# RWKV layer: the keys' input kept in SBUF as two parts, 1024-wide weight splits, no mask on the key products, factors padded to 112 rows, and weight loads issued by ScalarE

## The chip, the cores and the metric

The kernel runs on one core of one Trainium2 chip. The metric is the device time of one execution in microseconds (us): the median of three runs, and beside it one execution that was profiled. TensorE multiplies matrices, VectorE and GpSimd do elementwise work, ScalarE does activations, casts and copies, and SyncE (SP) issues most DMAs. Each engine takes its instructions in an order that is fixed when the program is built; DMAs of one issuing engine are issued in that engine's order too.

## The reference

Two layers over 256 positions of 2048 channels, in float32. Layer 0 mixes positions with Hyena and gated linear attention, layer 1 with RWKV-7; each is followed by a squared-ReLU feed-forward layer, and everything is modulated by a condition vector. The change lies in the RWKV block:

```python
xr, xw, xk, xv, xa, xg = [h + xx * mu[j] for j in range(6)]
r, k, v = heads(xr @ w_r), heads(xk @ w_k), heads(xv @ w_v)
kk = normalised(k * k_k)                            # per head of 64
for d in range(2):                                  # forward, backward
    logw = -0.606531 * sigmoid(w0[d] + tanh(xw @ w1[d]) @ w2[d])
    a = sigmoid(a0[d] + (xa @ a1[d]) @ a2[d])
    k_d = k * (1 + (a - 1) * k_a)
    state_out += rwkv7_scan(r, logw, k_d, v, kk, a)  # a state of 64x64 per head
    bonus += sum(r * k_d * r_k) * v
o = (groupnorm(state_out) + bonus) * g
return o @ w_o
```

## The kernel before

**Products in float32.** A factor `a` of a large product is split into `hi` (a cast to a TensorE format, by ScalarE, L466) and `lo = a - hi` (by VectorE, or GpSimd for inputs, L467). `prod` (L502) issues three matmuls, hi x hi, hi x lo and lo x hi (L505 to L507). A weight tile is 128 x 2 x 512 (512 KB); `load` (L488) takes it from DRAM with a DMA of SyncE into the pool `wp` of six buffers, which the background loads of the modulation weights (`ada`, L314 to L363) share.

**The order of the work.** The stages are generators; `weave` (L945) interleaves their steps by given counts, and a scheduler then fixes each engine's order from a simulated timeline. `issue_after(ins)` puts what is traced within it behind `ins` in its engine's order.

**The RWKV layer**, L1100 to L1271, in stages:

- *Norm and mixes.* `norm_steps` writes h; `xx` is the difference of the neighbours' mean and h. `spill_mixes` (L1275) makes the inputs of k, r and v, mixes 2, 0 and 3, two channel tiles (128 x 512 values) at a time with VectorE, and stores each to DRAM (`mix0`, `mix2`, `mix3`) with a DMA of SyncE. Beside it run the small projections (`lora`, L1284) and the first 35 steps of the projections.
- *Projections.* `rwkv_linear` (L1021) makes 512 output channels of k, r or v. It takes its tiles from `stream` (L994): for each of eight steps it loads an input tile `xu` (256 KB) back from DRAM, casts it (ScalarE) and subtracts (GpSimd), loads the next weight tile, and splits the present one in two halves of 512 columns (`split_weights`, `W1 = W2 = 2`). One input tile serves 24 matmuls. The same input is loaded and split again for each of the four blocks of output channels.
- *Keys.* In four rounds (L1171) the projections k and r of the next block run beside `rwkv_keys` (L1326) for the 16 pairs of heads, two lanes at a time, and `invert` (L1405) for the block before. Each two pairs load one tile of factors `up`, [97, 4, 256] (388 KB, L1180): 96 rows of w2 and a2 and a row of biases. For each direction `rwkv_keys` makes the decay (L1342 to L1344), `a` (L1347 to L1350), two tiles u0, u1 (VectorE and GpSimd), the cumulated decays (L1363 to L1365), the scaled factors `ab` (VectorE, L1374 to L1377, two products of 256 columns for the two tiles u), the products of 64 positions with each other (L1387), masked to the part below the diagonal by VectorE (L1393, `nm`), and stores them in `nd` and `ab` (L1394, L1395). `invert` reads `nd` in blocks of 32 rows (L1413) and uses the entries below the diagonal alone; `pair_load` reads back the blocks beside the diagonal.
- *Chain of states.* For pair after pair: `pair_load`, `pair_prep`, `pair_chain`, `pair_tail`, beside the other three blocks of v, then the output projection (`rwkv_out`, L1048). At the end (L1261) the last tile of each of the four output blocks is loaded, split, multiplied, and added to the residual.

The names in the profile: `tm_w`, `tm_wh`, `tm_wl` are a weight tile and its parts, `tm_xu`, `tm_xh`, `tm_xl` an input tile and its parts, `tm_up` the factors, `f_` the feed-forward layers, `tm_mm` and `tm_ps` PSUM tiles.

Of the kernel before, what the change touches and what calls it, by code (L numbers as in the profile page):

```python
# [16 lines left out]
P = 128  # L17
# [13 lines left out]
LG, MK, XS, TB, DU, RP, IB, L1, MP, AP = 2, 7, 4, 0, -8.0, 1, 3, 0, 3, 5  # L31
W1, W2, X1, X2 = 2, 2, 1, 1
BG, IV, CH, MT, B0, B1, M0, M1, LD = (10, 10, 10, 10, 10, 10, 10, 10, 10, 5, 5, 5, 5, 5, 5, 5, 5, 5), 12, 7, (5, 5, 5, 5, 5, 5, 5, 5, 5, 5, 5, 2, 3, 2, 3, 2, 3, 2), 3, 14, 6, 6, 6
PK = 8
RH, ZZ = (0, 2.4, 2, 2), 0
# [73 lines left out]
def _rwkv_constants():  # L109
    o = {}  # L110
    for d in range(2):
        st = _block_tri(64, True, d == 1)
        inc = _block_tri(64, False, d == 1)
        o[f"cum{d}"] = np.concatenate([st, inc], axis=1) * np.float32(-0.606531)
        st64, inc64 = st[:64, :64], inc[:64, :64]
        z = np.zeros((64, 64), np.float32)
        top = np.concatenate([z, inc64], axis=1)
        bot = np.concatenate([st64, inc64], axis=1)
        o[f"mm{d}"] = np.concatenate([bot, top] if d else [top, bot], axis=0)
    lower = np.tril(np.ones((64, 64), np.float32), -1)  # L120
    o["nm"] = np.concatenate([lower, lower], axis=0)
    h = np.arange(P) // 64
    o["bo"] = (h[:, None] == h[None, :]).astype(np.float32)
    return o


def layout(i):
# [56 lines left out]
    for n, v in _rwkv_constants().items():  # L184
        (rk1 if n[:3] in ("cum", "nm") else rk).add(n, v)
    a["rc"], a["rc1"] = rk.array(), rk1.array()
# [7 lines left out]
    for w, b in (("rw_w2", "rw_w0"), ("rw_a2", "rw_a0")):  # L194
        w, b = np.asarray(i[w])[0], np.asarray(i[b])[0]
        for d in range(2):
            up.append(np.concatenate([w[d], b[d][None]], axis=0))
    a["rw_up"] = np.stack(up, axis=1).reshape(97, 4, 8, T).transpose(2, 0, 1, 3)
    a["rw_g2"] = np.asarray(i["rw_g2"])[0].reshape(2, P, 4, NB).transpose(2, 1, 0, 3)
# [15 lines left out]
class Build:  # L215
# [21 lines left out]
    def run(self):  # L237
        nc, ctx, A = self.nc, self.ctx, self.A
        self.const = self.pool(ctx, "const")
        self.wp = self.pool(ctx, "wp", bufs=6)  # L240
        self.due, self.rate, self.turn, self.hold, self.starting = 0.0, 0.0, 0, None, False
        self.cut = None
# [12 lines left out]
        self.ada_next, self.ada_sum, self.ada_out, self.ada_done = [], {}, {}, {}  # L255
        self.label = self.stages[0]
        if self.stages[0] != "mix":
            self.start()
            self.load_x()
        for s in SUBS:  # L260
            if s in self.stages:
                self.label = s
                self.rate = RF0 if s == "f0" else RF1
                if s[0] == "f":
                    self.ffn(s)
                elif s == "mix":
                    self.mix()
                else:
                    self.rwkv()
        self.final()  # L270
# [194 lines left out]
    def split(self, a, hi, lo, eng=None):  # L465
        self.nc.scalar.copy(hi, a)  # L466
        d = (eng or self.nc.vector).tensor_tensor(lo, a, hi, ALU.subtract)  # L467
        if eng is None:
            self.cut = d.ins

    def behind(self):
# [16 lines left out]
    def load(self, name, n, i, pools):  # L488

        self.turn += 1  # L490
        w = self.t(pools[self.turn % len(pools)], [P, 2, NB], "w")
        self.dma = self.nc.sync.dma_start(w, self.A[name][n, i // 2][:, i % 2 * 2 : i % 2 * 2 + 2]).ins
        self.tick(self.rate / 2)
        return w
# [487 lines left out]

    def open_linear(self, st, bufs, fine, finex):
        self.fine, self.finex = fine, finex
        self.ws = self.pool(st, self.name("ws"), bufs=bufs, reuse_waits="tile")
        self.xt = self.pool(st, self.name("xt"), bufs=bufs, reuse_waits="tile")
# [7 lines left out]
    def stream(self, name, n, src, tiles):  # L994

        nc = self.nc
        w = [self.load(name, n, 0, [self.wp])]

        def ahead(i):
            u = self.t(self.xt, [P, 2, T], "xu", bufs=2)  # L1000
            nc.sync.dma_start(u, src[:, 2 * i : 2 * i + 2, :])
            x = [self.t(self.xt, [P, 2, T], t, dt=F32R) for t in ("xh", "xl")]
            for j in range(self.finex):
                c = slice(j * T // self.finex, (j + 1) * T // self.finex)
                self.split(u[:, :, c], *(a[:, :, c] for a in x), nc.gpsimd)
            if 2 * i + 2 < tiles:
                w.append(self.load(name, n, i + 1, [self.wp]))
            v = [self.t(self.ws, [P, 2, NB], t, dt=F32R) for t in ("wh", "wl")]
            self.split_weights(w[i], v)
            return x, v  # L1010
# [3 lines left out]
        for i in range(tiles // 2):  # L1014
            x, v = nxt
            if 2 * i + 2 < tiles:
                nxt = ahead(i + 1)
            for k in range(2):
                yield 2 * i + k, [a[:, k, :] for a in x], [a[:, k, :] for a in v]

# [79 lines left out]
    def rwkv(self):  # L1100
# [3 lines left out]
        xs = tc.dram_tile([P, 2, D], F32, name="x_spill")  # L1104
        self.xd = {j: tc.dram_tile([P, KT, T], F32, name=f"mix{j}") for j in (0, 2, 3)}
        yd = tc.dram_tile([P, KT, T], F32, name="y_spill")
# [6 lines left out]
        with ExitStack() as st:  # L1113
# [15 lines left out]
            st1 = st.enter_context(ExitStack())  # L1129
            self.open_linear(st1, 3, W1, X1)  # L1130
            rk = self.pool(st1, "rk", reuse_waits="tile")
# [17 lines left out]
            with ExitStack() as st2:  # L1149
# [11 lines left out]
                self.xstack.close()  # L1161
                self.rate = 0.0
                mixes = self.spill_mixes(h, xx)
# [5 lines left out]
            with st1:  # L1169
                p1 = self.pool(st1, "p1", reuse_waits="tile")  # L1170
                for n in range(4):  # L1171
# [3 lines left out]
                    def lane(o):  # L1175
                        for i in range(2):
                            p = 4 * n + 2 * i + o
                            if o == 0:
                                up[i] = self.t(p1, [97, 4, T], "up", bufs=2)
                                nc.sync.dma_start(up[i], A["rw_up"][p // 2])  # L1180
                            c = p % 4
                            yield from self.rwkv_keys(p1, p, r[:, c, :], k[:, c, :], kk[:, c, :], kh[:, c, :], up[i][:, :, o * P : (o + 1) * P])

# [6 lines left out]
            with ExitStack() as st1:  # L1190
                self.open_linear(st1, 2, W2, X2)
                p2 = self.pool(st1, "p2", reuse_waits="tile")
# [68 lines left out]
                for n in range(4):  # L1261
# [9 lines left out]
                    self.residual("tm", n, pts[n])  # L1271
        self.open_gate()
        self.open_work()

    def spill_mixes(self, h, xx):  # L1275
        for j in (2, 0, 3):
            for k in range(0, KT, 2):
                u = self.t(self.tmp, [P, 2, T], "u")
                for q in range(2):
                    self.mixed(h, xx, j, k + q, u[:, q, :])  # L1280
                self.nc.sync.dma_start(self.xd[j][:, k : k + 2, :], u)
                yield 1
# [43 lines left out]
    def rwkv_keys(self, rp, p, r, k, kk, kh, up):  # L1326
# [11 lines left out]
        for d in range(2):  # L1338
# [5 lines left out]
            Gp.tensor_scalar(sig, sig, 0.5, 0.5, ALU.mult, ALU.add)  # L1344
            th = self.t(rp, [P, T], "th", bufs=3)
            pt = self.pt([P, T])
# [5 lines left out]
            yield 1  # L1352
            u = [self.t(rp, [P, T], f"u{n}", bufs=3) for n in range(2)]
            V.scalar_tensor_tensor(u[d], th, 1.0, kh, ALU.add, ALU.mult)
            Gp.tensor_tensor(u[1 - d], sc, k, ALU.mult)
# [4 lines left out]
            en = self.t(rp, [P, T], "en", bufs=3)  # L1360
            pt = self.pt([P, 2, 2, P])
# [12 lines left out]
            V.tensor_tensor(ar[:, 0, :], ar[:, 0, :], kk, ALU.mult)  # L1374
            for n in range(2):
                V.tensor_tensor(bk[:, :, n, :], c4(u[n]), c4(en), ALU.mult)
            V.tensor_tensor(ar[:, 1, :], ar[:, 1, :], r, ALU.mult)  # L1377
# [14 lines left out]
            for hd in range(2):  # L1392
                V.tensor_tensor(nt[:, hd], pts[hd], self.rc("nm").unsqueeze(1).to_broadcast([P, 2, 64]), ALU.mult)  # L1393
            nc.sync.dma_start(self.nd[b][:, d, 256 * pb : 256 * pb + 256], nt.rearrange("p h t j -> p (h t j)"))  # L1394
# [319 lines left out]
```

## Time and profile before

| | us |
|---|---|
| median of three runs (3163.99 to 3170.43) | 3164.84 |
| the profiled execution | 3173.39 |
| its span, first to last instruction | 3171.6 |
| TensorE busy (matmuls) | 2904.6 |
| VectorE busy | 2195.9 |
| ScalarE busy | 1340.4 |
| GpSimd busy | 620.7 |

A profile row names the line, the engine (PE is TensorE, PEld its weight loads, DVE VectorE, ACT ScalarE, POOL GpSimd, SP SyncE; a q behind it is its sequencer, which waits and issues DMAs), the operation, what it writes and reads, its shape and count; then its busy time, the mean of one in ns, the engine's idle time just before it and what ended that. The granted clock is the share of TensorE's full clock that it was given. Busy time of overlapping instructions counts once in the views by stretches; in the groups each instruction counts with its full length, so matmuls that overlap add up to more.

### The profile page before, as it was taken

The page shows a single profiled execution, that of the slowest core. Times are in us where ns is not written, and L with a number is a line of the kernel's source. Part 1 is how long each engine was busy: PE and PEld are TensorE (multiplying, and loading weights), DVE is VectorE, ACT ScalarE, POOL GpSimd, SP SyncE. Part 2 cuts the span into 40 slices and gives each one's busy share as a digit, 9 for nine tenths or more (in the row PEclk, how much of TensorE's full clock was granted, in tenths as well). Part 3 has the DMA queues.
Part 4 walks back from the last instruction along what each step waited for, and adds up shares of the span by engine and source line. Part 5 has one row for each costly group of instructions (what it writes and reads, how often), then busy time and mean ns, then how long its engine had stood idle before and what let it go on. Part 6 is the DMA issues. An engine that isn't in the chain of part 4 may idle for free. (4 is left out here: it accounts for less than half of the span.)

```text
span 3171.6 us, 52610 instructions
## 1 busy us (share of the span) xinstructions
PE 2904.6 (92%) x20308; PEld 2513.1 (79%) x20308; DVE 2195.9 (69%) x3350; ACT 1340.4 (42%) x2083; POOL 620.7 (20%) x646
## 2 busy tenths in 40 slices
PE   5999899999999999979577777999998999999998
PEld 2677776799988998868476676787777998899986
DVE  7899776657777787787368685975556677555554
ACT  3233444444433444433354553444445444344443
POOL 1211100021100110023355464442323110001100
PEclk9999999999999999999788897998999999999999
DMA  9978777648889888966455567896635678555552
GB/s 320 326 257 290 245 269 265 230 150 285 291 305 314 291 295 301 311 214 226 152 185 175 178 208 192 270 292 208 192 108 192 224 250 284 196 188 180 199 193 99
DMA packets 285494, 741.39 MB, mean 234 GB/s; under 512 B 73601, under 2 KB 100097, under 8 KB 284092
## 3 DMA queue, kind: packets, MB, share of 16 engines
q1 hardware_dynamic: 284668, 734.40, 69.0%
q8 instruction: 159, 2.61, 0.3%
q10 hardware_dynamic: 576, 3.64, 0.3%
q14 instruction: 91, 0.75, 0.1%
HBM read 697.23 MB, written 40.70 MB: 233 GB/s over the span
## 5 line engine op out<-in xcount | busy, mean ns | idle before, releaser
L467 DVE TENSOR_TENSOR f_wl<-f_w,f_wh 128x1024 fp32r<-128x1024 f32 x512 | 631.0, 1233 | 444.5 <-ACT f_wh L466 440.4
L466 ACT CAST f_wh<-f_w 128x1024 fp32r<-128x1024 f32 x512 | 538.4, 1052 | 748.3 <-PE f_mm L507 319.3
L506 PE MATMUL f_mm<-f_h,f_wh 128*128 128x256 f32 x2048 | 579.6, 283 | 0.0
L505 PE MATMUL f_mm<-f_h,f_wh 128*128 128x256 f32 x2048 | 579.4, 283 | 0.0
L507 PE MATMUL f_mm<-f_h,f_wl 128*128 128x256 f32 x2048 | 579.0, 283 | 0.0
L506 PE MATMUL f_mm<-f_wl,f_hid 128*128 128x512 f32 x1024 | 398.6, 389 | 0.6 <-DVE f_wl L467 0.6
L507 PE MATMUL f_mm<-f_wh,f_hid 128*128 128x512 f32 x1024 | 398.5, 389 | 0.0
L506 PEld LDWEIGHTS f_mm<-f_h,f_wh 128*128 128x128 f32 x2048 | 393.2, 192 | 0.2
L505 PEld LDWEIGHTS f_mm<-f_h,f_wh 128*128 128x128 f32 x2048 | 393.0, 192 | 0.1
L507 PEld LDWEIGHTS f_mm<-f_h,f_wl 128*128 128x128 f32 x2048 | 392.9, 192 | 0.0
L505 PE MATMUL f_mm<-f_wh,f_hid 128*128 128x512 f32 x1024 | 357.9, 389 | 0.0
L467 POOL TENSOR_TENSOR f_hid<-f_u,f_hid 128x512 fp32r<-128x512 f32 x64 | 98.0, 1531 | 990.0 <-ACT f_hid L466 985.2
L467 DVE TENSOR_TENSOR tm_wl<-tm_w,tm_wh 128x512 fp32r<-128x512 f32 x256 | 206.0, 830 | 99.0 <-ACT tm_wh L466 98.4
L363 DVE SCALAR_TENSOR_TENSOR mix_w<-mix_w,mix_s 128x1024 f32<-128x1024 f32 x175 | 219.8, 1265 | 73.3 <-DMA mix_w<-in_ada_f 49.1
L505 PE MATMUL tm_mm<-tm_xh,tm_wh 128*128 128x256 f32 x768 | 242.9, 320 | 18.5 <-ACT tm_xh L466 11.1
L506 PE MATMUL tm_mm<-tm_xl,tm_wh 128*128 128x256 f32 x768 | 234.5, 306 | 8.8 <-POOL tm_xl L467 8.8
L363 DVE SCALAR_TENSOR_TENSOR f_w<-f_w,mix_s 128x1024 f32<-128x1024 f32 x174 | 233.4, 1344 | 2.3 <-DMA f_w<-in_ada_f 2.3
L507 PE MATMUL tm_mm<-tm_xh,tm_wl 128*128 128x256 f32 x768 | 232.6, 305 | 1.4 <-DVE tm_wl L467 1.4
L467 POOL TENSOR_TENSOR tm_xl<-tm_xu,tm_xh 128x512 fp32r<-128x512 f32 x113 | 169.4, 1500 | 310.5 <-ACT tm_xh L466 268.8
L506 PEld LDWEIGHTS f_mm<-f_wl,f_hid 128*128 128x128 f32 x1024 | 192.2, 188 | 40.9 <-DVE f_wl L467 1.2
L507 PEld LDWEIGHTS f_mm<-f_wh,f_hid 128*128 128x128 f32 x1024 | 192.2, 188 | 39.8
L505 PEld LDWEIGHTS f_mm<-f_wh,f_hid 128*128 128x128 f32 x1024 | 192.3, 188 | 39.7
(445 smaller groups left out, 5413.9 us busy)
## 6 DMA issues: line engine op xcount, KB each, us to landing
f_w<-in_w SPq DMA_DIRECT2D x512, 512.0 KB, 4.9
f_w<-in_ada_f SPq DMA_DIRECT2D x125, 512.0 KB, 5.5
mix_w<-in_ada_mix SPq DMA_DIRECT2D x96, 512.0 KB, 6.4
mix_w<-in_w_in SPq DMA_DIRECT2D x80, 512.0 KB, 5.2
mix_w<-in_ada_f SPq DMA_DIRECT2D x64, 512.0 KB, 5.0
f_w<-in_ada_tm SPq DMA_DIRECT2D x49, 512.0 KB, 5.7
tm_xu<-mix SPq DMA_DIRECT2D x96, 256.0 KB, 4.8
mix_w<-in_w_out SPq DMA_DIRECT2D x32, 512.0 KB, 4.7
```

The lines of the kernel that those rows point to most:

```text
L363: V.scalar_tensor_tensor(w, w, 1.0, self.s[:, j * (D // 2) : (j + 1) * (D // 2)], ALU.mult, ALU.mult, accum_out=a[:, j, i : i + 1])
L466: self.nc.scalar.copy(hi, a)
L467: d = (eng or self.nc.vector).tensor_tensor(lo, a, hi, ALU.subtract)
L505: mm(out, lhsT=l[0], rhs=r[0], start=start, stop=False)
L506: mm(out, lhsT=l[0], rhs=r[1], start=False, stop=False)
L507: mm(out, lhsT=l[1], rhs=r[0], start=False, stop=stop)
```

## The change

- The padded factors: `rw_up` gets 15 rows of zeros, and the tile `up` is [112, 4, 256]; the products read its first 97 rows.
- The inputs: `spill_mixes` splits each mix once. The parts of the keys' input stay in two SBUF tiles (`xk`); those of r and v are stored to DRAM together, 512 KB for two channel tiles, and `stream` loads them back as they are, without a cast or a subtract.
- Weight splits are one cast and one subtract of 1024 columns (`W1 = W2 = 1`), and `stream` loads `PF = 3` weight tiles ahead of the one that it splits, not one.
- In the RWKV layer, from the spill of x to its end, `load` issues the weight DMAs from ScalarE, behind the newest cast of a weight (`casts[-1]`), and not from SyncE. This holds for the output projection too, where a load is traced one tile ahead.
- The mask is gone: ScalarE copies the products of L1387 whole.
- In `rwkv_keys` u0 and u1 are one tile, and their product with `en` is one operation over 512 columns; `th` and `en` have two buffers, not three.

```diff
-W1, W2, X1, X2 = 2, 2, 1, 1
+W1, W2 = 1, 1
-PK = 8
+PK, PF = 8, 3
...
-    a["rw_up"] = np.stack(up, axis=1).reshape(97, 4, 8, T).transpose(2, 0, 1, 3)
+    up = np.stack(up, axis=1).reshape(97, 4, 8, T).transpose(2, 0, 1, 3)
+    a["rw_up"] = np.concatenate([up, np.zeros((8, 15, 4, T), np.float32)], axis=1)
...
     def split(self, a, hi, lo, eng=None):
-        self.nc.scalar.copy(hi, a)
+        c = self.nc.scalar.copy(hi, a)
         d = (eng or self.nc.vector).tensor_tensor(lo, a, hi, ALU.subtract)
         if eng is None:
             self.cut = d.ins
+            self.casts = [c.ins]
...
-        self.dma = self.nc.sync.dma_start(w, self.A[name][n, i // 2][:, i % 2 * 2 : i % 2 * 2 + 2]).ins
+        src = self.A[name][n, i // 2][:, i % 2 * 2 : i % 2 * 2 + 2]
+        if self.wq is None:
+            self.dma = self.nc.sync.dma_start(w, src).ins
+        else:
+            with self.tc.issue_after(self.casts[-1]):
+                self.wq.dma_start(w, src)
...
-        w = [self.load(name, n, 0, [self.wp])]
+        w = [self.load(name, n, i, [self.wp]) for i in range(PF)]
 
         def ahead(i):
-            u = self.t(self.xt, [P, 2, T], "xu", bufs=2)
-            nc.sync.dma_start(u, src[:, 2 * i : 2 * i + 2, :])
-            x = [self.t(self.xt, [P, 2, T], t, dt=F32R) for t in ("xh", "xl")]
-            for j in range(self.finex):
-                c = slice(j * T // self.finex, (j + 1) * T // self.finex)
-                self.split(u[:, :, c], *(a[:, :, c] for a in x), nc.gpsimd)
-            if 2 * i + 2 < tiles:
-                w.append(self.load(name, n, i + 1, [self.wp]))
+            if isinstance(src, list):
+                x = src[i // 4][:, 2 * i % 8 : 2 * i % 8 + 2]
+            else:
+                x = self.t(self.xt, [P, 2, 2, T], "x", bufs=self.xb, dt=F32R)
+                nc.sync.dma_start(x.bitcast(F32), src[:, 2 * i : 2 * i + 2])
+            if 2 * (i + PF) < tiles:
+                w.append(self.load(name, n, i + PF, [self.wp]))
...
-            self.open_linear(st1, 3, W1, X1)
+            self.open_linear(st1, 3, W1, 3)
+            xk = self.pool(st1, "xk", reuse_waits="tile")
+            self.xd[2] = [self.t(xk, [P, 8, 2, T], f"xk{i}", dt=F32R) for i in range(2)]
...
-                self.rate = 0.0
+                self.rate, self.wq = 0.0, nc.scalar
...
-                                up[i] = self.t(p1, [97, 4, T], "up", bufs=2)
+                                up[i] = self.t(p1, [112, 4, T], "up", bufs=2)
...
-                self.nc.sync.dma_start(self.xd[j][:, k : k + 2, :], u)
+                if j == 2:
+                    x = self.xd[2][k // 8][:, k % 8 : k % 8 + 2]
+                else:
+                    x = self.t(self.hp, [P, 2, 2, T], "xs", bufs=2, dt=F32R)
+                self.split(u, x[:, :, 0], x[:, :, 1], self.nc.gpsimd)
+                if j != 2:
+                    self.nc.sync.dma_start(self.xd[j][:, k : k + 2], x.bitcast(F32))
...
-            for n in range(2):
-                V.tensor_tensor(bk[:, :, n, :], c4(u[n]), c4(en), ALU.mult)
+            V.tensor_tensor(bk, u.rearrange("p n (c t) -> p c n t", t=64), c4(en).unsqueeze(2).to_broadcast([P, 4, 2, 64]), ALU.mult)
...
-                V.tensor_tensor(nt[:, hd], pts[hd], self.rc("nm").unsqueeze(1).to_broadcast([P, 2, 64]), ALU.mult)
+                S.copy(nt[:, hd], pts[hd])
```

More of the change, by code (lines that the diff above doesn't have):

```diff
@@ L119, in _rwkv_constants @@
         o[f"mm{d}"] = np.concatenate([bot, top] if d else [top, bot], axis=0)
-    lower = np.tril(np.ones((64, 64), np.float32), -1)
-    o["nm"] = np.concatenate([lower, lower], axis=0)
     h = np.arange(P) // 64
@@ L184, in layout @@
     for n, v in _rwkv_constants().items():
-        (rk1 if n[:3] in ("cum", "nm") else rk).add(n, v)
+        (rk1 if n[:3] == "cum" else rk).add(n, v)
     a["rc"], a["rc1"] = rk.array(), rk1.array()
@@ L241, in run @@
         self.due, self.rate, self.turn, self.hold, self.starting = 0.0, 0.0, 0, None, False
-        self.cut = None
+        self.cut, self.casts, self.wq = None, [], None
         self.small = self.pool(ctx, "small", bufs=2)
@@ L981, in mixed, with open_linear @@
         self.nc.vector.scalar_tensor_tensor(o, xx[k // 8][:, k % 8, :], self.v(f"mu{j}")[:, k : k + 1], h[k // 8][:, k % 8, :], ALU.mult, ALU.add)
-    def open_linear(self, st, bufs, fine, finex):
-        self.fine, self.finex = fine, finex
+    def open_linear(self, st, bufs, fine, xb):
+        self.fine, self.xb = fine, xb
         self.ws = self.pool(st, self.name("ws"), bufs=bufs, reuse_waits="tile")
@@ L1018, in stream @@
             for k in range(2):
-                yield 2 * i + k, [a[:, k, :] for a in x], [a[:, k, :] for a in v]
+                yield 2 * i + k, [x[:, k, a] for a in range(2)], [a[:, k, :] for a in v]
     def rwkv_linear(self, name, n, j, out):
@@ L1104, in rwkv @@
         xs = tc.dram_tile([P, 2, D], F32, name="x_spill")
-        self.xd = {j: tc.dram_tile([P, KT, T], F32, name=f"mix{j}") for j in (0, 2, 3)}
+        self.xd = {j: tc.dram_tile([P, KT, 2, T], F32, name=f"mix{j}") for j in (0, 3)}
         yd = tc.dram_tile([P, KT, T], F32, name="y_spill")
@@ L1178, in lane @@
                             if o == 0:
-                                up[i] = self.t(p1, [97, 4, T], "up", bufs=2)
+                                up[i] = self.t(p1, [112, 4, T], "up", bufs=2)
                                 nc.sync.dma_start(up[i], A["rw_up"][p // 2])
                             c = p % 4
-                            yield from self.rwkv_keys(p1, p, r[:, c, :], k[:, c, :], kk[:, c, :], kh[:, c, :], up[i][:, :, o * P : (o + 1) * P])
+                            yield from self.rwkv_keys(p1, p, r[:, c, :], k[:, c, :], kk[:, c, :], kh[:, c, :], up[i][:97, :, o * P : (o + 1) * P])
                     def late():
@@ L1190, in rwkv @@
             with ExitStack() as st1:
-                self.open_linear(st1, 2, W2, X2)
+                self.open_linear(st1, 2, W2, 3)
                 p2 = self.pool(st1, "p2", reuse_waits="tile")
@@ L1271, in rwkv @@
                     self.residual("tm", n, pts[n])
+        self.wq = None
         self.open_gate()
@@ L1344, in rwkv_keys @@
             Gp.tensor_scalar(sig, sig, 0.5, 0.5, ALU.mult, ALU.add)
-            th = self.t(rp, [P, T], "th", bufs=3)
+            th = self.t(rp, [P, T], "th", bufs=2)
             pt = self.pt([P, T])
@@ L1352, in rwkv_keys @@
             yield 1
-            u = [self.t(rp, [P, T], f"u{n}", bufs=3) for n in range(2)]
-            V.scalar_tensor_tensor(u[d], th, 1.0, kh, ALU.add, ALU.mult)
-            Gp.tensor_tensor(u[1 - d], sc, k, ALU.mult)
+            u = self.t(rp, [P, 2, T], "u2", bufs=3)
+            V.scalar_tensor_tensor(u[:, d], th, 1.0, kh, ALU.add, ALU.mult)
+            Gp.tensor_tensor(u[:, 1 - d], sc, k, ALU.mult)
             ab = self.t(rp, [P, 1024], "ab", bufs=4)
@@ L1359, in rwkv_keys @@
             bk = ab[:, 512:].rearrange("p (c n t) -> p c n t", c=4, n=2)
-            en = self.t(rp, [P, T], "en", bufs=3)
+            en = self.t(rp, [P, T], "en", bufs=2)
             pt = self.pt([P, 2, 2, P])
```

## The prediction

> **What bounds the kernel now.** I read the time and the slices first, then the busy time by stretches of the RWKV layer, then who waited for whom in the worst stretch, then the SyncE queue there. In the slices the TensorE row has one long dip, slices 20 to 25, and its granted clock drops with it:
>
> ```profile
> span 3171.6 us, 52610 instructions
> PE   5999899999999999979577777999998999999998
> PEclk9999999999999999999788897998999999999999
> ```
>
> One slice is 3171.6/40 = 79.3 us, so this is about 1507 to 1982 us: the keys stage, in which the heads' factors are made (`rwkv_keys`) beside the projections k, r and the first block of v. The busy time by stretches (us, then busy us and instruction count of each engine, granted clock, DMA share, GB/s):
>
> ```profile
> 1385.00:1505.00 120.00, 103.61 (x644) 91.24 (x645) 92.68 (x165) 41.56 (x72) 44.86 (x42) 0.95 0.64 215
> 1505.00:1562.00 57.00, 30.61 (x220) 28.95 (x219) 19.46 (x32) 18.17 (x38) 18.57 (x23) 0.73 0.43 139
> 1955.00:2160.00 205.00, 196.27 (x2271) 164.67 (x2272) 156.54 (x351) 85.34 (x216) 82.19 (x96) 0.92 0.91 270
> 2160.00:2420.00 260.00, 254.07 (x2702) 194.27 (x2702) 151.87 (x325) 120.69 (x305) 73.16 (x107) 0.99 0.53 161
> 1505.00:1955.00 450.00, 319.64 (x2442) 287.68 (x2440) 300.27 (x566) 209.57 (x420) 222.92 (x276) 0.83 0.56 181
> ```
>
> The columns are TensorE, its weight loads, VectorE, ScalarE, GpSimd. The mixes (1385 to 1505) and the chain of states (1955 to 2420) have TensorE busy for 86% and 97%. In the keys stage no engine is full: TensorE has 319.6 of 450 us, VectorE 300.3, the DMA engines 56%. 130 us of TensorE are idle there, and its clock is 0.83. So this stage is bound by waits. They are, for TensorE, ScalarE and VectorE in turn (total us, times, longest):
>
> ```profile
> PE tm_ps L1387 <- DVE tm_ab L1376: 40.2, 13, 6.6
> PE tm_ps L1317 <- ACT tm_u L1315: 23.9, 3, 10.5
> PE tm_mm L1387 <- DVE tm_ab L1376: 16.3, 3, 11.5
> PE tm_ps L1342 <- DMA tm_up<-in_rw_up: 14.9, 1, 14.9
> PE tm_mm L505 <- ACT tm_bon L1401: 7.4, 1, 7.4
> PE tm_mm L505 <- ACT tm_xh L466: 5.9, 2, 3.2
> ACT tm_xh L466 <- DMA tm_xu<-mix: 124.4, 27, 14.9
> DVE tm_wl L467 <- ACT tm_wh L466: 69.0, 12, 13.5
> ```
>
> They are one chain: TensorE waits for VectorE and ScalarE, VectorE waits for ScalarE's casts, and ScalarE, which takes its instructions in order, stands for 124 us in front of the cast of an input tile `xu` that has not landed. Why a 256 KB tile lands late is in the SyncE queue (start, us to issue):
>
> ```profile
> 1505.26 5.37 SPq L1180 DMA_DIRECT2D tm_up<-in_rw_up  x2
> 1510.73 14.68 SPq L492 DMA_DIRECT2D tm_w<-in_rw_k  x1
> ...
> 1616.35 0.31 SPq L1180 DMA_DIRECT2D tm_up<-in_rw_up  x1
> 1616.76 4.40 SPq L1001 DMA_DIRECT2D tm_xu<-mix  x1
> 1621.27 13.09 SPq L1413 DMA_DIRECT2D tm_E<-nd  x4
> ```
>
> The factors' load `up` of 1616.35 is itself issued in 0.31 us. Behind it and its fellows the next issues take 14.68, 4.40 and, for four, 13.09. The first `up`, 388 KB, goes out at 1505.26; its first reader starts at 1524.6, after the 14.9 us wait shown above: 19.3 us, where a 512 KB weight tile needs 5.7 (median to landing):
>
> ```profile
> L1342 PEld LDWEIGHTS tm_ps<-tm_up,tm_hw x104: 186/192/338, 1524.6 to 1911.3; 97*128 97x128 f32 x104
> tm_w<-in_rw_r SPq DMA_DIRECT2D x32, 512.0 KB, 5.7
> tm_w<-in_rw_o SPq DMA_DIRECT2D x32, 512.0 KB, 4.5
> tm_up<-in_rw_up SPq DMA_DIRECT2D x8, 388.0 KB
> ```
>
> So `up` moves at 20 GB/s, beside 92 for a weight tile that shares the engines with others, and a stage that moves 181. I read it as a transfer that goes through one of the 16 DMA engines, with every later transfer waiting for its share of that engine. There are eight of them, one for each 56 us of the stage. The Trainium skill, "DMA: Bandwidth & Descriptors", section on why a DMA increments its semaphore by 16, has the rule for it: a transfer uses the largest number of engines up to 16 that divides its slowest dimension, so 97 rows use one and 112 would use all 16. The trace agrees for 97; for 112 no run here shows it.
>
> **The change part by part.** The rows for the terms (busy us, mean ns; the first seven of the keys stage, then a matmul of the feed-forward layers, one ScalarE issue, a wait of the SyncE queue over the RWKV layer, and a 1024-wide subtract of the feed-forward layers):
>
> ```profile
> L467 DVE TENSOR_TENSOR tm_wl<-tm_w,tm_wh 128x512 fp32r<-128x512 f32 x120 | 101.4, 869 | 69.1 <-ACT tm_wh L466 69.0
> L1376 DVE TENSOR_TENSOR tm_ab<-tm_u,tm_en 128x256 f32<-128x256 f32 x64 | 33.2, 554 | 2.4 <-POOL tm_u L1355 2.4
> L1393 DVE TENSOR_TENSOR tm_N<-tm_ps,tm_rc 128x128 f32<-128x128 f32 x48 | 12.8, 280 | 7.4 <-PE tm_ps L1387 6.4 <-PE tm_mm L1387 1.0
> L466 ACT CAST tm_wh<-tm_w 128x512 fp32r<-128x512 f32 x118 | 67.2, 621 | 18.4 <-PE tm_mm L506 18.1
> L466 ACT CAST tm_xh<-tm_xu 128x512 fp32r<-128x512 f32 x57 | 35.3, 621 | 131.1 <-DMA tm_xu<-mix 124.4 <-PE tm_mm L507 3.7 <-POOL tm_kr L1398 3.0
> L467 POOL TENSOR_TENSOR tm_xl<-tm_xu,tm_xh 128x512 fp32r<-128x512 f32 x58 | 88.6, 1530 | 151.8 <-ACT tm_xh L466 133.9 <-issue 15.3 <-DMA ab<-tm_ab 2.5
> L505 PE MATMUL tm_mm<-tm_xh,tm_wh 128*128 128x256 f32 x479 | 152.4, 321 | 13.3 <-ACT tm_bon L1401 7.4 <-ACT tm_xh L466 5.9
> L505 PE MATMUL f_mm<-f_h,f_wh 128*128 128x256 f32 x2048 | 579.4, 283 | 0.0
> L1160 ACTq DMA_DIRECT2D x_spill<-mix_x x1: 333/333/333, 1381.2 to 1381.2; - x1
> SPq L492 <- DVE tm_wl L467: 93.6, 42, 13.6
> L467 DVE TENSOR_TENSOR f_wl<-f_w,f_wh 128x1024 fp32r<-128x1024 f32 x512 | 631.0, 1233 | 444.5 <-ACT f_wh L466 440.4
> ```
>
> *Keys stage, the waits.* The factors' load gets 112 rows. Its cost afterwards lies between today's 19.3 us and that of a weight tile; I take the weight tile, 5.7, as it is the same size and kind. The inputs also stop being cast here: keys read SBUF, r and v come as finished parts, so TensorE alone waits for them and ScalarE no longer stands in front of a DMA. Of TensorE's waits above I strike the `up` load (14.9), those on ScalarE (23.9, 7.4, 5.9 = 37.2) and half of those on VectorE at L1387 (56.5/2 = 28), which VectorE owes to late casts; the other half is the lanes' own latency and stays. That is 80 us. Late next is VectorE. Its bounds: 52 us (no VectorE wait goes) and 108 (all do).
>
> *Keys stage, the clock.* A projection's matmul takes 321 ns here and 283 where TensorE runs without gaps. With 283 for 321 throughout, 319.6 us would be 282, 38 less; the gaps do not all close, so I take 15, with 0 and 38 as ends.
>
> *Keys stage, the engines' work.* VectorE: 60 weight tiles as one subtract of 1233 instead of two of 869 save 60 x 0.505 = 30 us; 64 masks of 0.28 save 18; one product over 512 for two over 256 saves about 32 x (1.108 - 0.869) = 8. It keeps 244 us, so it does not bound a stage of 355. ScalarE: 57 input casts go (-35), 64 mask copies come (at the mask's own 0.28, +18), 60 issues of 0.333 come (+20), and wider casts are at worst equal: about 213 us, no bound. GpSimd loses 88.6. All this I count at nothing beyond the waits. Two small tiles, `th` and `en`, go from three buffers to two; each is read within a step, so I count nothing, and if a lane does wait it is for one product, 0.55 us. The inputs of r and v still go through the SyncE queue, behind stores that wait for VectorE, but three tiles ahead instead of two.
>
> *Mixes, 1385 to 1505.* 24 casts and 24 GpSimd subtracts come, 16 each of the projections' own go, so +8 x 0.62 us on ScalarE and +8 x 1.53 on GpSimd, which have 78 and 75 us free beside 104 us of TensorE; 16 wider splits save 8 us of VectorE. The stores of the mixes for r and v go out one cast and one subtract, 2.2 us, later, and nothing reads them for a whole projection. I take 0, with 8 either way.
>
> *Chain of states.* TensorE is busy 97% there and loses no matmul, so cheaper splits bring nothing. Two things cost. The inputs of the three later v blocks come as 512 KB, not 256: 24 tiles, +6.3 MB in a stretch that moves 270 GB/s at a share of 0.91, so up to 297 at full share: 21 us of DMA against 18 free. I take 5, between 0 and 21. And ScalarE now issues the weight loads behind its newest cast. In the projections that cast is three tiles back, in the output's loop two; but at the end, where four output tiles follow each other, a load stands directly behind the cast of the tile before: 0.33 to issue, 4.5 to land, two casts of 0.62 make 6.1 us for a tile. Today these loads go out well ahead, the last at 2395, and are cast from 2409 on:
>
> ```profile
> 2392.90 2.48 SPq L492 DMA_DIRECT2D tm_w<-in_rw_o  x2
> ...
> 2409.30 2.18 ACT L466 CAST tm_wh<-tm_w 128x512 fp32r<-128x512 f32 x4 [4.47 <-PE tm_ps L507]
> ...
> 2414.09 1.14 ACT L466 CAST tm_wh<-tm_w 128x512 fp32r<-128x512 f32 x2 [1.14 <-PE tm_mm L507]
> ```
>
> Three tiles cast within 5.9 us become three of 6.1 each: +12; some of it hides behind the residual, so 10, between 0 and 15. What queues behind ScalarE's waits there are the copies of the chain (L1551, L1561, L1578), for which TensorE waits next.
>
> A rule against this part stands in the same page of the Trainium skill, section "Issuing engines are not separate DMA queues": a second issuing engine saves only issue time. By it the move to ScalarE earns nothing by itself; my sum credits it nothing either, and the wait at the end remains.
>
> The sum, against the profiled execution: -80 - 15 + 0 + 5 + 10 = -80 us. The profiled execution took 3173.4 (span 3171.6), 8.6 above the median of the runs, 3164.8; the difference goes on the median: 3085.
>
> **The rivals.** *The factors' load is not the cause, or stays slow*: if ScalarE's late tiles come from the order of the SyncE queue and the lanes' own latency, TensorE only gains the first wait and some of ScalarE's, about 14.9 + 25 of the 37, and pays the 15 of the chain: 3140. For it: much of the waiting stands at L1387, a short chain through three engines. Against it: the long waits of ScalarE, up to 14.9 us, are as long as the stuck issues.
>
> *VectorE becomes the bound and all waits go*: the stage shrinks to TensorE's 282 us plus the lanes' starts, about 300: -150 + 15, 3030. For it: VectorE's 244 and TensorE's 282 both fit. Against: TensorE's order is fixed and a lane passes four engines at each step.
>
> *Slower*: ScalarE inherits the wait of the SyncE queue. The weight loads waited 93.6 us there for VectorE to release a slot of the pool of six; now ScalarE stands in front of them, and behind it the cast that VectorE needs next and the copies of the chain. With all 93.6 on the path beside -80 the change ends at +14, 3179. It decides from 80 us of such waits on. Against it: the load stands behind a cast three tiles back, so its slot has usually been free for two tiles; only in the stretch 1955 to 2160, where the gate's 35 background tiles share the pool, is it tight.
>
> **How the numbers follow.** My forecast has 0.66. Its terms' ends, 28 either way for the waits, 19 for the clock and 13 for the chain, are independent and add in squares to 36, so its own range is 3049 to 3121. The small gain has 0.15, the large one 0.11, slower 0.06, and 0.02 that gains and costs meet within 0.2% (6.3 us, about what a measurement of this kernel can tell from no change). Faster is then 0.92, the same 0.02, slower 0.06. The range over the cases, leaving out slower and the far ends of the others, is 3025 to 3145.
>
> **What would show it.** In the profile after, `up` should land within some 6 us and no issue behind it should take over 3; ScalarE's wait for `mix` tiles should be gone; slices 19 to 24 should show TensorE at 8 or 9 and a clock near 0.9; the keys stage should last about 355 us, the chain about 480, with a gap in TensorE before the last four output tiles. I am wrong if ScalarE shows long waits in front of weight loads, if TensorE's waits at L1387 stay at 56 us, or if the chain's stretch grows by more than 30 us.

## The result and the profile after

| | before | after |
|---|---|---|
| median, us, on one chip | 3166.76 | 3079.90 |
| ratio, 95% interval | | 0.972 (0.970 to 0.974) |
| the profiled execution, us | 3173.39 | 3078.22 |
| its span, us | 3171.6 | 3076.4 |

The forecast was 3085. Three disturbed executions count in the medians but not in the ratios: one of the changed kernel (3230.86 us, at a clock of 0.835), and one each of e1 and e5 below (4637.7 and 9578.1 us); without them the medians are 3079.2, 3118.1 and 3069.5.

The page of the changed kernel: the span, and the rows of TensorE and of its granted clock in 40 slices of 76.9 us.

```profile
span 3076.4 us, 51944 instructions
PE   5998989999999999998999969899998999999998
PEclk9999999999999999998999988799999999999999
```

The long dip of slices 20 to 25 is gone. A short one is left in slices 24 to 26 (TensorE 6, 9, 8, clock 8, 8, 7), 1769 to 2000 us: the end of the keys stage and the first two fifths of the chain.

To compare stages exactly I cut at TensorE's own landmarks: the first matmul of the norm, the last of `lora`, the first and the last of the line with which `pair_chain` begins (L1549 before, L1561 after), and the first of the next norm.

| stage, us | before | after | difference |
|---|---|---|---|
| mixes | 118.4 | 119.7 | +1 |
| keys | 453.0 | 324.8 | -128 |
| chain of states | 394.2 | 419.0 | +25 |
| output tail | 75.6 | 81.5 | +6 |
| feed-forward after it | 743.3 | 743.8 | 0 |

The busy time by stretches for keys, chain and tail (us; then busy us and count of TensorE, its weight loads, VectorE, ScalarE, GpSimd; granted clock, DMA share, GB/s), before:

```profile
1505.00:1958.00 453.00, 319.64 (x2442) 287.68 (x2440) 300.43 (x566) 209.57 (x420) 223.87 (x278) 0.83 0.56 181
1958.00:2353.00 395.00, 386.43 (x4645) 310.51 (x4646) 266.82 (x613) 174.03 (x458) 137.84 (x189) 0.95 0.73 217
```

and after:

```profile
1507.30:1832.10 324.80, 280.66 (x2412) 257.26 (x2410) 240.89 (x409) 184.20 (x362) 150.14 (x218) 0.95 0.81 260
1832.10:2251.20 419.10, 391.20 (x4650) 314.35 (x4651) 256.58 (x581) 160.43 (x408) 103.62 (x170) 0.91 0.70 212
2251.20:2332.60 81.40, 67.72 (x329) 50.63 (x329) 39.78 (x59) 36.73 (x60) 18.93 (x15) 0.94 0.59 193
```

Two subtractions in each row say what happened. Keys: TensorE's idle time fell from 453.0 - 319.6 = 133 us to 324.8 - 280.7 = 44, and its busy time by 39, for the same matmuls at a clock of 0.95 and not 0.83. (The trace holds 1417 of the projections' matmuls after and 1439 before; at some 0.3 us each, up to 7 of the 39 can be missing records.) Chain: idle rose from 9 to 28 us, busy time by 5 at a clock of 0.91.

The factors' tile after, its first reader, its issue, and its landing (smallest, median, longest):

```profile
L1355 PEld LDWEIGHTS tm_ps<-tm_up,tm_hw x104: 186/192/337, 1516.7 to 1783.4; 97*128 97x128 f32 x104
...
L1186 SPq DMA_DIRECT2D tm_up<-in_rw_up x8: 338/364/949, 1507.2 to 1721.0; - x8
...
DMA to landing us min/median/max: 5.1/7.6/10.3
```

The first reader starts 9.5 us after the issue, not 19.3. What TensorE waited for, keys stage and then chain (total us, times, longest):

```profile
PE tm_ps L1399 <- DVE tm_ab L1388: 19.6, 9, 5.1
PE tm_ps L1376 <- POOL tm_sig L1357: 8.4, 6, 3.6
PE tm_mm L1512 <- DMA tm_bk<-ab: 8.2, 1, 8.2
```

```profile
PE tm_ps L1561 <- ACT tm_Q L1590: 11.0, 4, 7.2
PE tm_ps L1616 <- ACT tm_Q L1573: 5.6, 1, 5.6
PE tm_mm L1582 <- ACT tm_Q L1573: 3.0, 1, 3.0
```

The longest in the chain before was this one, for GpSimd:

```profile
PE tm_ps L1549 <- POOL tm_M L1496: 4.0, 1, 4.0
```

In the keys stage, the waits for `up` and for ScalarE's `u`, `xh` and `bon` are gone from the head of the list; the lanes' own latency at the 64-position products (L1399, before L1387) stays with 20 us. In the chain the idle time has a new releaser: ScalarE's `Q`, 20 us in these three rows, as much as the idle time grew.

### The profile page after: what moved, and what is told of

Its sections match the earlier page's. It is cut to its first block, busy times and chain, and to the rows that moved or that the text cites. A ratio compares the mean times of both kernels' runs of the same rounds, so it can differ in the third digit from the quotient of the medians.

```text
span 3076.4 us, 51944 instructions
## 1 busy us (share of the span) xinstructions
PE 2881.3 (94%) x20308; PEld 2497.0 (81%) x20308; DVE 2121.1 (69%) x3126; ACT 1303.2 (42%) x1947; POOL 524.6 (17%) x574
## 5 line engine op out<-in xcount | busy, mean ns | idle before, releaser
L466 DVE TENSOR_TENSOR tm_wl<-tm_w,tm_wh 128x1024 fp32r<-128x1024 f32 x128 | 165.0, 1289 | 106.9 <-ACT tm_wh L465 103.5
L465 ACT CAST mix_wh<-mix_w 128x1024 fp32r<-128x1024 f32 x114 | 119.4, 1050 | 202.8 <-PE mix_mm L512 89.3
L466 DVE TENSOR_TENSOR mix_wl<-mix_w,mix_wh 128x1024 fp32r<-128x1024 f32 x114 | 142.4, 1254 | 38.9 <-ACT mix_wh L465 38.8
L510 PE MATMUL tm_mm<-tm_x,tm_wh 128*128 128x256 f32 x512 | 160.5, 314 | 6.5 <-DMA tm_x<-mix 4.8
L465 ACT CAST tm_wh<-tm_w 128x1024 fp32r<-128x1024 f32 x128 | 133.6, 1044 | 77.1 <-PE tm_mm L511 33.5
```

The source lines that it names most:

```text
L465: c = self.nc.scalar.copy(hi, a)
L510: mm(out, lhsT=l[0], rhs=r[0], start=start, stop=False)
```

## The experiments

The theory after the result: the factors' slow load was the root of the keys stage's waits, ready-made input parts take away what is left of ScalarE's, the other parts of the change earn next to nothing, and issuing loads from ScalarE is what the chain and the tail pay for. Against it stood these rivals: that the parts alone make the gain, that more rows help by their number and not by its factors, that v's larger inputs slow the chain, and that three tiles ahead fill the pool's slots. Times are medians; ratios are to the kernel before on the same chip. Stages are cut as above. No experiment changes what is computed.

| run | median, us | ratio (interval) | keys | chain | tail |
|---|---|---|---|---|---|
| after | 3079.9 | 0.972 (0.970 to 0.974) | 325 | 419 | 81 |
| e1 padding alone | 3119.3 | 0.983 (0.980 to 0.986) | 381 | 409 | 76 |
| e2 all but padding | 3158.0 | 0.995 (0.994 to 0.997) | 411 | 406 | 84 |
| e3 loads by SyncE | 3054.8 | 0.963 (0.960 to 0.966) | 333 | 392 | 74 |
| e4 SyncE from the chain on | 3050.7 | 0.961 (0.959 to 0.964) | 333 | 390 | 74 |
| e5 splits of 512 | 3070.5 | 0.967 (0.965 to 0.969) | 323 | 410 | 79 |
| e6 mask back | 3075.2 | 0.969 (0.967 to 0.971) | 327 | 412 | 82 |
| e7 padding and parts | 3063.9 | 0.965 (0.962 to 0.967) | 338 | 396 | 76 |
| e8 one ahead in the chain | 3091.0 | 0.974 (0.972 to 0.975) | 340 | 412 | 82 |
| e9 101 rows | 3163.8 | 0.998 (0.997 to 0.999) | 413 | 412 | 82 |
| e10 loads by GpSimd | 3080.8 | 0.972 (0.970 to 0.973) | 341 | 408 | 74 |
| e11 e4 with splits of 512 | 3051.9 | 0.963 (0.961 to 0.965) | 334 | 386 | 76 |
| e12 ScalarE, not behind the cast | 3092.0 | 0.976 (0.974 to 0.977) | 340 | 423 | 74 |

### The padding: e1, e2, e9

e1 is the kernel before with 15 rows of zeros and nothing else:

```diff
-                                up[i] = self.t(p1, [97, 4, T], "up", bufs=2)
+                                up[i] = self.t(p1, [112, 4, T], "up", bufs=2)
```

> The kernel before with one edit: the factors' tile gets 112 rows instead of 97. Theory (the factors' load on one DMA engine causes most of the waiting in the keys stage): the load lands within about 8 us, ScalarE's 124 us of waiting for mix tiles falls below 50, the keys stage gets 60 to 80 us shorter, 3085 to 3105 us in all. Rival (the late tiles come from the order of the SyncE queue and the casts of the inputs): only the first wait of 14.9 us and some of ScalarE's go, 3130 to 3152.

Measured: 3119.3, between the two. `up` landed in 6.2 us (median), and the keys stage lost 72 us. The keys and the chain by stretches:

```profile
1509.10:1890.10 381.00, 307.86 (x2440) 280.86 (x2438) 306.09 (x565) 207.56 (x415) 228.23 (x276) 0.87 0.70 218
1890.10:2298.60 408.50, 391.49 (x4644) 314.84 (x4644) 267.84 (x613) 175.17 (x462) 131.26 (x190) 0.93 0.70 208
```

What ScalarE still waited for in the keys stage, with the old inputs:

```profile
ACT tm_xh L467 <- DMA tm_xu<-mix: 35.3, 17, 6.4
```

Of the 124 us, 89 went with the padding alone: most of these waits stood behind the factors' load, not behind the inputs' own. The total fell less than the keys stage because the chain came out 14 us longer, although nothing in it was edited; TensorE's idle time in it was 17 us. So I take some 10 us either way of a chain's length to belong to how the order of the whole program falls. The keys stage varies likewise: e4 and e8 (below) are edited only behind it, and show 333 and 340 where the changed kernel shows 325. Smaller differences of a stage are not read below.

e2 is the changed kernel with 97 rows:

```diff
-    a["rw_up"] = np.concatenate([up, np.zeros((8, 15, 4, T), np.float32)], axis=1)
+    a["rw_up"] = up
```

> The changed kernel with the factors' tile back at 97 rows, all else kept. Theory: the keys stage gets the stuck transfers back, now in front of weight tiles and the inputs of r and v, 40 to 70 us, 3120 to 3150 in all. Rival (dropping the input casts did it): the first wait of 15 us comes back and little else, 3090 to 3100.

Measured: 3158.0, 8 above the theory's range. All the rest of the change together is worth 0.5% without the padding. The keys stage takes 411 us, 86 more than with it, and the waits come back, now on TensorE itself:

```profile
PE tm_ps L1399 <- DVE tm_ab L1388: 28.4, 10, 15.5
PE tm_mm L510 <- DMA tm_x<-mix: 25.5, 5, 10.3
PE tm_ps L1355 <- DMA tm_up<-in_rw_up: 14.6, 1, 14.6
PE tm_mm L1512 <- DMA tm_bk<-ab: 11.1, 1, 11.1
```

Three of the four rows are DMAs. The inputs `x` cost 25.5 us, where the changed kernel waits 1.7 us for them, and `up` itself 14.6: a slow load harms its neighbours more than its own readers. (The wait for `bk` is no sign of it, the changed kernel has one of 8.2 us too.) That the parts alone make the gain is refuted.

e9 asks whether it is the number of rows or its factors: 101 rows, four more than 97, and prime as 97 is.

```diff
-    a["rw_up"] = np.concatenate([up, np.zeros((8, 15, 4, T), np.float32)], axis=1)
+    a["rw_up"] = np.concatenate([up, np.zeros((8, 4, 4, T), np.float32)], axis=1)
...
-                                up[i] = self.t(p1, [112, 4, T], "up", bufs=2)
+                                up[i] = self.t(p1, [101, 4, T], "up", bufs=2)
```

> The changed kernel with the factors' tile at 101 rows: four rows of zeros more than 97, eleven fewer than 112. Theory (the number of rows decides how many DMA engines share the load, and a prime number leaves one): as slow as with 97 rows, 3150 to 3166, the load at 18 to 22 us. Rival (the load was slow for its place in the queue or its odd size, and fewer bytes than 112 rows can only help): as fast as the changed kernel, 3074 to 3090.

Measured: 3163.8, keys 413 us. The keys stage, the SyncE queue at its start, and the first reader:

```profile
1509.70:1922.70 413.00, 304.15 (x2477) 278.84 (x2475) 241.08 (x411) 185.82 (x368) 146.51 (x221) 0.85 0.64 215
```

```profile
1509.56 6.40 SPq L1186 DMA_DIRECT2D tm_up<-in_rw_up  x2
```

```profile
L1355 PEld LDWEIGHTS tm_ps<-tm_up,tm_hw x104: 186/192/333, 1534.3 to 1858.8; 97*128 97x128 f32 x104
```

The reader starts 24.7 us after the issue; with 112 rows 9.5. The loads land 20.6 to 25.7 us after their issue, and the second of the first pair after 43.9, most of them above the 18 to 22 expected. Four more rows alone do not help.

The trace shows the mechanism itself, for it records every update of the semaphore (a counter that others wait on) that tells of a load's landing. Each of the eight `up` loads leaves 16 updates with 112 rows, and two with 97 rows (the kernel before and e2) or 101: the first right after the issue, the last when the load has landed. In the kernel before, a load of 49 rows (`mix_b<-in_gla_up`) leaves eight, and one of a single row two. I read this as one update for each DMA engine that took part, and one more for all the others, if there are any: one engine for 97 and for 101 rows, seven for 49, and 16 for 112. A mere threshold in rows would not give 49 rows more engines than 101. What a load on one engine does to others stands in the same record. In the kernel before, two `up` loads are issued at 1505.26 and 1505.60 and land 19.2 and 36.2 us later. The loads issued behind them, from the same record (us; updates counted from the start of each issue):

| issued at | load | first 15 updates | the last |
|---|---|---|---|
| 1510.72 | weight tile of k (issue 14.68) | 17.1 to 17.9 | 32.3 |
| 1525.51 | weight tile of r | 3.7 to 5.2 | 18.8 |
| 1525.97 | input tile `xu` | 6.0 to 6.6 | 19.0 |
| 1530.29 | weight tile of r | 3.9 to 5.4 | 16.0 |
| 1547.08 | input tile `xu` | 2.0 to 2.7 | 2.8 |

In the first four rows fifteen parts of a tile are there within 1.5 us of each other, and the sixteenth comes 11 to 14 us later: it stood behind the `up` loads. Once the second `up` has landed, at 1541.8, and what stood behind it is through, a tile is whole in 2.8 us. So 112 helps by its factors. That is the divisor rule of the Trainium skill, "DMA: Bandwidth & Descriptors", section "Why a DMA increments its semaphore by 16 and not by 1": it gives one engine to 97 and to 101 rows and 16 to 112, and the runs agree.

### The inputs as parts: e7

e7 is the kernel before with the padding and the parts (keys' input in SBUF, those of r and v read back as parts), and nothing else of weight; seen from the changed kernel:

```diff
-W1, W2 = 1, 1
+W1, W2 = 2, 2
-PK, PF = 8, 3
+PK, PF = 8, 1
...
-                self.rate, self.wq = 0.0, nc.scalar
+                self.rate, self.wq = 0.0, None
...
-            V.tensor_tensor(bk, u.rearrange("p n (c t) -> p c n t", t=64), c4(en).unsqueeze(2).to_broadcast([P, 4, 2, 64]), ALU.mult)
+            for n in range(2):
+                V.tensor_tensor(bk[:, :, n, :], c4(u[:, n]), c4(en), ALU.mult)
...
-                S.copy(nt[:, hd], pts[hd])
+                V.tensor_tensor(nt[:, hd], pts[hd], self.rc("nm").unsqueeze(1).to_broadcast([P, 2, 64]), ALU.mult)
```

> The kernel before with two parts of the change: padded factors and the inputs kept as finished parts (the keys' in SBUF). Splits of 512, the mask, one weight tile ahead and loads by SyncE stay. Theory (what is left after the padding comes from ScalarE no longer casting inputs in front of DMAs): the keys stage falls from 381 us with the padding alone to 335 to 350, 3060 to 3080 in all. Rival (the wider splits, the mask and the deeper loading bring it): 3095 to 3120.

Measured: 3063.9, keys 338, chain 396: these two parts make more than the whole change does.

```profile
1508.20:1846.40 338.20, 292.44 (x2465) 267.82 (x2463) 260.77 (x568) 182.03 (x367) 140.89 (x221) 0.93 0.81 257
```

From e1 the parts take 43 us off the keys stage (381 to 338). Everything else takes 13 more (338 to 325), no more than this stage varies by, and the chain is 23 longer with it.

### What lies under cover: e5, e6

e5 splits weights in two halves again (`W1, W2 = 2, 2`), e6 gives the mask back to VectorE:

```diff
-                S.copy(nt[:, hd], pts[hd])
+                V.tensor_tensor(nt[:, hd], pts[hd], self.rc("nm").unsqueeze(1).to_broadcast([P, 2, 64]), ALU.mult)
```

> The changed kernel with the weight splits back at two of 512 columns. Theory (VectorE has room in the keys stage, so its work there is cover): 0 to 8 us slower than the changed kernel, 3078 to 3090 in all. Rival (with the stuck transfers gone VectorE is close to the bound there): the 30 us of VectorE come back for the greater part, 3095 to 3112.

> The changed kernel with the key products masked by VectorE again instead of copied whole by ScalarE. Theory (cover): within 5 us of the changed kernel. Rival (VectorE close to the bound): 64 masks of 0.28 us cost 10 to 18 us, 3090 to 3098.

Measured: 3070.5 and 3075.2, keys 323 and 327 against 325. VectorE's 64 masks and its narrower subtracts are hidden, as the 241 us it is busy out of 325 let one expect. e5 came out 8 us below its theory's range, 0.6% faster than the change: the wider splits earn nothing. Its chain is 9 us shorter, within what a chain varies by.

### Who issues the loads: e3, e4, e8, e10, e11, e12

```diff
-                self.rate, self.wq = 0.0, nc.scalar
+                self.rate, self.wq = 0.0, None
```

> The changed kernel with all weight loads of the RWKV layer issued by SyncE again, three tiles ahead as in the change. Theory (ScalarE issuing them earns nothing in the keys stage, and in the chain of states it makes ScalarE wait for slots of the weight pool behind late background tiles, some 25 us): the keys stage stays within 6 us, the chain gets 15 to 30 us shorter, 3050 to 3068. Rival (taking the loads off the SyncE queue is what frees the keys stage): 20 us or more slower than the changed kernel, 3100 or more.

> The changed kernel with the weight loads issued by SyncE from the chain of states on, and by ScalarE up to it. Theory: the chain's 25 us over the kernel before and the output's 6 come back in most part, 3050 to 3068. Rival (the larger inputs of v, 512 KB for 256, fill the DMA engines there): nothing changes, 3074 to 3086.

e3 leaves all loads to SyncE (the diff above); e4 only from the chain on (`self.wq = None` once the keys are made). Measured: 3054.8 and 3050.7. Chain and tail are back at 392 and 390, 74 and 74, below the kernel before, with v's 512 KB inputs in both: the larger inputs cost nothing that these runs can tell. ScalarE's issuing earns nothing clear in the keys stage (333 without it; 325, 333 and 340 with it) and costs 27 to 29 in the chain and 8 in the tail. Over all kernels the six chains whose loads SyncE issues take 386 to 409 us, 395 in the mean, the eight with a second issuing engine 406 to 423, in the mean 413: about 18 of the 27 are the issuing engine's, the rest may be variation. The Trainium skill, "DMA: Bandwidth & Descriptors", section "Issuing engines are not separate DMA queues", says that a second issuing engine saves only issue time. These runs agree that it brings no more; here it costs as well.

Where it costs stands in ScalarE's own rows in the chain of the changed kernel (start, us; in brackets the idle time before and its releaser):

```profile
1970.28 0.34 ACTq L497 DMA_DIRECT2D tm_w<-in_rw_v  x1
1970.67 0.27 ACT L1573 ACTIVATE tm_Q<-tm_ps 64x128 f32<-64x128 f32 x1 [7.87 <-DMA tm_pc<-ab]
1976.53 0.34 ACTq L497 DMA_DIRECT2D tm_w<-in_rw_v  x1
1976.91 0.27 ACT L1573 ACTIVATE tm_Q<-tm_ps 64x128 f32<-64x128 f32 x1 [5.97 <-DMA tm_w<-in_ada_tm]
...
2049.28 0.33 ACTq L497 DMA_DIRECT2D tm_w<-in_rw_v  x1
2049.66 0.30 ACT L1590 COPY tm_Q<-tm_S 64x128 f32<-64x128 f32 x1 [9.22 <-DMA tm_r<-ab]
```

The issue takes 0.34 us. But ScalarE stood still ahead of it for 7.9, 6.0 and 9.2 us, until transfers had landed that SyncE had issued, and that neither the load nor the copy to `Q` has anything to do with: the chain's `pc`, a weight of the modulation, and the chain's `r`. Behind each is a copy for which TensorE waits:

```profile
1970.99 0.48 PE L1616 MATMUL tm_ps<-tm_M,tm_Q 128*64 128x64 f32 x4 [5.56 <-ACT tm_Q L1573]
...
1977.24 0.69 PE L1582 MATMUL tm_mm<-tm_Q,tm_bkt 128*64 128x64 f32 x4 [3.05 <-ACT tm_Q L1573]
...
2050.01 0.70 PE L1561 MATMUL tm_ps<-tm_Q,tm_M 128*64 128x64 f32 x8 [7.25 <-ACT tm_Q L1590]
```

These three are 15.9 of the 19 us by which TensorE's idle time in the chain grew. In the trace the instruction that holds ScalarE just ahead of the issue waits on the semaphore that counts the load's own landing; SyncE's and ScalarE's DMAs share eight of these. All 33 loads that ScalarE issues in the chain go out after the transfer that last used their semaphore has landed, and these three within 0.1 us of it. So I read it as a load that may not go out before that transfer has landed. That the wait is there is shown; this cause of it is read from the semaphores, and e10 below bears on it. In the chain of e3, where ScalarE issues no weight load, its longest wait for a transfer is 1.8 us:

```profile
ACT tm_wh L465 <- DMA tm_X<-rx: 1.8, 1, 1.8
```

Two other readings were tried. e8 loads one tile ahead in the chain, not three, so that fewer slots of the pool are taken:

```diff
-        w = [self.load(name, n, i, [self.wp]) for i in range(PF)]
+        pf = PF if self.lag == L1 else 1
+        w = [self.load(name, n, i, [self.wp]) for i in range(pf)]
```

(and `pf` for `PF` in `ahead`).

> The changed kernel, but from the chain of states on the weights of v are loaded one tile ahead, not three; ScalarE still issues them. Theory A (ScalarE waits for a slot of the weight pool, which three tiles ahead and five background tiles overfill): the pool fits again, the chain gets 15 to 27 us shorter, 3053 to 3066. Theory B (the trace names the landing of other DMAs of SyncE, such as the 2 KB tile pc, as what ends ScalarE's wait in front of its issue, so that wait does not depend on the slots): the chain stays within 8 us, 3072 to 3088.

Measured: 3091.0, 3 above theory B's range, since keys came out at 340. The chain is 412, 7 us shorter, no more than chains vary by, and the total is not better. Slots are not what the chain pays for. e12 leaves the loads on ScalarE, but not behind the cast:

```diff
-            with self.tc.issue_after(self.casts[-1]):
-                self.wq.dma_start(w, src)
+            self.wq.dma_start(w, src)
```

> The changed kernel with the weight loads issued by ScalarE without being tied to its newest cast; the scheduler places them. Theory: ScalarE's waits in front of its issues stay, so the chain stays at 405 to 425; the output gets its early loads back, 73 to 78 us instead of 81.5; 3066 to 3084 in all. Rival (the tie to the cast makes the loads late, and that is the whole loss of the chain): the chain falls to 390 to 398, 3045 to 3060.

Measured: 3092.0, above the theory's range, since keys came out at 340. The chain stays long, 423 us, with the same kind of wait:

```profile
ACT tm_Q L1572 <- DMA tm_w<-in_ada_tm: 10.6, 1, 10.6
```

and the tail returns to 74. So the place behind the cast costs the tail, and not the chain. e10 gives the loads to GpSimd:

```diff
-                self.rate, self.wq = 0.0, nc.scalar
+                self.rate, self.wq = 0.0, nc.gpsimd
```

> The changed kernel with the weight loads of the RWKV layer issued by GpSimd, not by ScalarE; they are then not tied to the newest cast. Theory B (in the chain ScalarE stands in front of its own issues until unrelated DMAs of SyncE have landed): ScalarE's waits for DMAs go, the chain falls from 419 to 390 to 400 us, 3050 to 3068 in all. Rival (any second issuing engine makes the loads late there): the chain stays at 410 or more, 3076 or more.

Measured: 3080.8, in the rival's range. In this trace GpSimd's loads have eight semaphores of their own, and none of the 32 in the chain goes out within 0.1 us of the landing of the transfer that used its semaphore before. ScalarE's waits for foreign transfers are gone in the chain but for one of 1.3 us (8.4 us are left, for its own `xu`), as they should be if the shared semaphores made them. The tail is 74, but the chain is still 408 us. TensorE then waits for ScalarE's `Q` 9.3 us in all, and 16.6 us idle at a clock of 0.91 remain. So either ScalarE's waits are not the whole cost of a second issuing engine, or this is a long chain by the 10 us that chains vary by: e1, whose loads SyncE issues, has 409. Which, stays open.

e11 joins the best pieces: SyncE from the chain on, splits of 512.

> Weight loads by SyncE from the chain of states on, as in the fourth run, and splits of 512 columns. Theory (the 512 splits gained in the chain because the first half of a tile reaches TensorE earlier where ScalarE's waits make tiles late; without these waits there is nothing to gain): 3048 to 3062, the keys stage within 6 us of 333 and the chain of 390. Rival (shorter instructions of ScalarE and VectorE help the chain itself): 10 us or more faster than the fourth run, below 3042.

Measured: 3051.9, the same as e4. e4 and e11 beat both kernels: e4 by 3.9% the one before, and the change by about 1.1% (0.961/0.972; each ratio is to the kernel before on its own chip), with intervals that do not meet.

## Why the prediction was right, and which terms were mis-sized

- **The factors' load as the root: right.** e1, e2 and e9 show it by doing the padding alone, leaving it out, and spoiling it, and the semaphores show the reading behind it: one engine for `up`, and in every transfer behind it one part that waits for that engine. "Within some 6 us" was 7.6 in the median, 6.2 in e1. That no issue behind it would take over 3 us was wrong: the longest wait of an issue there was 13.8, for VectorE's `ab` (L1407). SyncE still waits for producers, it only no longer makes others late.
- **Waits of the keys stage, -80: measured -89** (idle 133 to 44), within its bounds. The half of the waits at the 64-position products that was to stay, 28, is 20.
- **The clock, -15: measured about -39**, the upper end. This is the term that was mis-sized. I reasoned that the gaps would not all close; but they need not, the clock was back at 0.95 with 44 us still idle. Over the runs it rises as the idle time of the stage falls: 0.83 at 133 us, 0.85 at 109 (e9), 0.87 at 73 (e1), 0.93 at 46 (e7); below 50 us the order is lost (0.93 at 39 in e11). The trace's own record has the clock at full or at half, in steps of 3.41 us: at half for 152 us of the stage before, and for 35 after. The Trainium skill, "TensorE: Matmul & The Clock Gate", Part 1, halves the clock after an idle window of about 3.4 us. That would make the long gaps the ones that count, and the rows agree in part: TensorE's longest waits here were 14.9, 11.5 and 10.5 us before, and 8.2, 5.1 and 3.6 after; but in e11 none was over 4.2, and the clock was at half for 46 us all the same. The two terms together, -95 by forecast, were -128.
- **Work of the engines at nothing: right.** VectorE kept 241 us (244 by forecast), and giving its work back made nothing slower (e5, e6). ScalarE kept 184, not 213: the issues don't count as busy, and the wider cast took 1.05 us, less than two of 0.62.
- **Mixes, 0: right**, +1.
- **Chain and tail, +15: measured +31.** v's larger inputs, +5, were 0 (e3, e4). The tail, +10, was +6: a tile took 3.8 to 4.8 us, not 6.1, as the starts of its casts show:

```profile
2307.50 1.04 ACT L465 CAST tm_wh<-tm_w 128x1024 fp32r<-128x1024 f32 x1
2311.34 1.05 ACT L465 CAST tm_wh<-tm_w 128x1024 fp32r<-128x1024 f32 x1 [2.80 <-DMA tm_w<-in_rw_o]
...
2315.39 1.05 ACT L465 CAST tm_wh<-tm_w 128x1024 fp32r<-128x1024 f32 x1 [3.00 <-DMA tm_w<-in_rw_o]
...
2320.22 1.04 ACT L465 CAST tm_wh<-tm_w 128x1024 fp32r<-128x1024 f32 x1 [0.44 <-DMA tm_w<-in_rw_o]
```

  What was missing is +25 in the chain from the issuing engine. The slower rival had the right place, ScalarE standing in front of loads with the chain's copies behind, but the wrong reason, slots (e8), and about a quarter of its price (25 of 93.6 us).
- **The signs of being wrong.** Two of the three that the prediction named did come: ScalarE shows long waits in front of weight loads, up to 9.2 us, and the chain's stretch with the tail grew by 31 us, over the 30 named. Both concern the issuing engine; there the prediction was wrong, for it priced the tail and not the chain. The third, the waits at the 64-position products, fell from 56 us to 20.
- **The sum**, -80, was -95 in the span: 33 more gained in the keys stage, 16 more lost in the chain and tail, 2 lost elsewhere. Of the errors, half cancelled. Against the medians the change made -87 (3166.8 to 3079.9), since the profiled execution of before ran 6.6 above that median and the one after 1.7 below its own. So the forecast of 3085 is nearer to the median than its terms were to theirs, and that it missed by 5 us only is in part luck.

## What to carry to other kernels

Where a stage has no full engine and a low clock, look for one transfer that moves far slower than others of its size and for what is issued behind it; a row count that 16 divides, as it does 112, then comes first: here it took 72 us off the stage by itself, and without it all rearranging of the work around it was worth 0.5%. Price a closed gap twice, once as idle time and once as clock: here 89 and 39 us. And before moving DMA issues to a compute engine, ask what that engine will stand in front of: here an issue of 0.34 us held it for up to 9.

## What was not expected of the hardware

Four rows more than 97 cost as much as 97 (25 us to the first reader), 15 more bring 9.5; and of the transfers behind the slow load it was one part in sixteen that came late. And a load on a second issuing engine waited, with its engine, for up to 12.3 us (e5) until transfers of the first had landed that it shares no data with.
